# Attention values as 128 stationary columns (high beside low), with the two halves added in SBUF

## The chip, the cores and the metric

One core of a Trainium2 chip runs the whole program. The metric is the time of one execution on the device in microseconds (us): median 2431.57 us of 3 runs (2431.19 to 2432.11). TensorE is written PE (PEld is its weight load), VectorE DVE, ScalarE ACT, GpSimd POOL. Each engine takes its instructions from its own queue.

## The reference, cut to what matters

A two-layer decoder trunk on x (1, 256, 2048): retention, ConvFFN, sliding-window attention, ConvFFN, all in float32. The change is in the attention: 32 query heads of 64 columns share 4 key and value heads, two blocks of 128 tokens, window 128.

```
proj = h @ w_qkv + b_qkv; q, k, v = split(proj)
scores = q k^T * 64**-0.5 - slope * dist        (own block and the block before)
scores = where(valid, scores, -inf)
probs = softmax(concat(scores, sink))[..., :-1]
out = probs @ v;  return out @ w_out
```

## The kernel before, in words

Every wide product is made of three float32r products: an operand x is split in hi (x rounded to float32r) and lo = x - hi, and hi·hi, hi·lo and lo·hi are summed in PSUM. The weights come from HBM in units of 128 x 2048 (tile raw); ACT writes hi (L161), DVE writes lo (L162), 1024 columns at a time. PE runs the chunks of these units in one long stream: L267 and L269 for the projections that come out transposed, L256 to L258 for the others.

The rest is cut into generators ("tasks"). After each chunk `run_main` calls `split_ahead`, which may emit the next L161 and L162, and then `run_tasks`, which runs every task that is due, in order of due time. A task that yields n is due again n steps later (a step is one chunk of 512 columns, or two of 256). `tc.manual_schedule()` keeps the order of emission, so every engine's queue has the order in which this loop wrote it, and it does not depend on times.

Two query heads make a pair; 16 pairs, `att_pair`, come 4 steps apart: pairs 1 to 10 while the query columns 0 to 4 and the first output product run, pairs 11 to 16 while columns 5 to 7 and the second output product run. The stages of one pair, and the step in which they are emitted:

- step 0: scores on PE into two PSUM tiles (L679).
- step 1: DVE adds the ALiBi term and takes the maximum, with PSUM as input (L687), then L693 and L694.
- step 2: ACT takes the exponentials, four with their sums (L699), then L703.
- step 4: DVE adds the sink, inverts (L705, L706) and scales the probabilities (L710).
- step 6: PE transposes them, three per head into one PSUM tile each (L276); ACT and DVE split them into pT hi and lo (L400, L401).
- step 9: PE multiplies by the values into PSUM tile po (L393, inside `split_products`, called from `att_pair`), and ACT copies po to y (L731, L732).
- step 10: ACT and DVE split y into yT hi and lo (L400, L401).

Three pairs are under way at a time. In a stretch of 4 steps the queues hold, by the trace:

```
ACT: L731 L732 (pair n), L161, L400 yT (n), L400 pT x2 (n+1), L699 x4 and L703 (n+2), [L378], L161, [L638 x2]
DVE: L705 L706 L710 x4 (n+1), L687 x4 L693 L694 (n+2), L162, L401 yT (n), L401 pT x2 (n+1), [L379 L388], L162
```

In brackets: the eviction of a finished block of query columns (L378, L379, L388, L638), in every second stretch while query columns run. The PSUM tiles of this phase (`ms`, four slots) are taken in turn: two score tiles, po, two transpose tiles, and again.

`split_products` gives three matmuls, each with 64 stationary columns (one value head, hi or lo) and the probabilities as moving operand: for each head three of 256 moving columns (keys of block 0) and three of 128 (keys of block 1), 12 in all. `att_values` makes the values once, before the pairs.

Of the kernel before, what the change touches and what calls it, by code (L numbers as in the profile page):

```python
# [9 lines left out]
F32 = mybir.dt.float32  # L10
F32R = mybir.dt.float32r
AF = mybir.ActivationFunctionType
ALU = mybir.AluOpType
# [3 lines left out]
P = 128  # L17
D = 2048
S = 256
NT = S // P  # L20
# [3 lines left out]
KV = 4  # L24
GRP = 8
DH = 64
# [83 lines left out]
class Kernel:  # L110
# [533 lines left out]
    def att_values(self, at, g):  # L644
        v = self.ph.tile([P, NT, 256], F32, tag="qT", name="v", bufs=2)
        for t in range(NT):
            self.nc.vector.scalar_tensor_tensor(
                out=v[:, t], in0=g.ps[:, t, :256], scalar=self.r[:, t : t + 1], in1=self.bv,
                op0=ALU.mult, op1=ALU.add,
            )  # L650
        at["vs"] = x = self.ph.tile([P, 2, NT, 256], F32R, tag="vs", name="vs")
        self.nc.scalar.copy(out=x[:, 0], in_=v)
        self.nc.vector.tensor_tensor(
            out=x[:, 1], in0=v, in1=x[:, 0].bitcast(F32), op=ALU.subtract
        )

    def att_queries(self, at, b, g):
        qT = self.join(g, "qT", 2)
# [5 lines left out]
    def att_pair(self, at, qT, i, f):  # L664

        nc = self.nc
        kT, vs = at["kT"], at["vs"]
        jj = f // GRP
        al = self.ph.tile([P, 2, 384], F32, tag="al", name="al", bufs=2)
        nc.sync.dma_start(out=al, in_=self.a["alibi"][f])  # L670
        pr = self.ph.tile([P, 2, 384], F32, tag="pr", name="pr", bufs=3)
        soft = self.st.tile([P, 4, NT, 2], F32, tag="soft", name="soft")
        m, nm, es, den = (soft[:, x] for x in range(4))
        pss = [self.ms.tile([P, 512], F32, tag="ms", name="ms") for _ in range(2)]
        where = [slice(0, P), slice(P, P + S)]
        for t in range(NT):
            for s in range(2):
                rows = slice(s * DH, (s + 1) * DH)
                nc.tensor.matmul(  # L679
                    pss[s][:, where[t]], lhsT=qT[rows, i, t * P : (t + 1) * P],  # L680
                    rhs=kT[rows, jj, : (t + 1) * P], start=True, stop=True,
                )
        yield 1
        for s in range(2):
            sink = self.sinks[:, 2 * f + s : 2 * f + s + 1]
            for t in range(NT):
                nc.vector.tensor_tensor_reduce(  # L687
                    out=pr[:, s, where[t]], in0=pss[s][:, where[t]], in1=al[:, s, where[t]],
                    scale=DH**-0.5, scalar=sink, op0=ALU.add, op1=ALU.max,
                    accum_out=m[:, t, s : s + 1],  # L690
                )
        sk = self.sinks[:, 2 * f : 2 * f + 2].unsqueeze(1).broadcast_to([P, NT, 2])
        nc.vector.tensor_scalar_mul(nm, m, -1.0)  # L693
        nc.vector.tensor_tensor(out=es, in0=sk, in1=m, op=ALU.subtract)  # L694
        yield 1
        for s in range(2):
            for t in range(NT):
                x = pr[:, s, where[t]]
                nc.scalar.activation(  # L699
                    out=x, in_=x, func=AF.Exp, bias=nm[:, t, s : s + 1],  # L700
                    accum_out=den[:, t, s : s + 1],
                )
        nc.scalar.activation(out=es, in_=es, func=AF.Exp)  # L703
        yield 2
        nc.vector.tensor_tensor(out=den, in0=den, in1=es, op=ALU.add)  # L705
        nc.vector.reciprocal(den, den)  # L706
        for s in range(2):
            for t in range(NT):
                x = pr[:, s, where[t]]
                nc.vector.tensor_scalar_mul(x, x, den[:, t, s : s + 1])  # L710
        yield 2
        pTs = []
        for s in range(2):
            ps = self.ms.tile([P, 512], F32, tag="ms", name="ms")
            self.transposes(ps, [pr[:, s, n * P : (n + 1) * P] for n in range(3)])
            pT = self.ph.tile([P, 2, 384], F32R, tag="pT", name="pT", bufs=2)
            self.split_store(pT.unsqueeze(1), ps[:, :384].unsqueeze(1))
            pTs.append(pT)
        yield 3
        po = self.ms.tile([P, 2, S], F32, tag="ms", name="po")  # L720
        for s in range(2):
            vc = slice((2 * jj + s) * DH, (2 * jj + s + 1) * DH)
            pT = pTs[s]
            self.split_products(
                po[:DH, s], vs[:, :, 0, vc], pT[:, :, :S], start=True, stop=False
            )
            self.split_products(
                po[:DH, s, P:], vs[:, :, 1, vc], pT[:, :, S:], start=False, stop=True
            )
        y = self.ph.tile([P, S], F32, tag="y", name="y", bufs=2)  # L730
        nc.scalar.copy(out=y[:DH], in_=po[:DH, 0])  # L731
        nc.scalar.copy(out=y[DH:], in_=po[:DH, 1])  # L732
        yield 1
        self.attT[f] = x = self.ph.tile([P, 2, S], F32R, tag="yT", name="yT", bufs=12)
        self.split_store(x.unsqueeze(1), y.unsqueeze(1))

# [221 lines left out]
```

## Time and profile before

| | |
|---|---|
| profiled execution, its own time | 2431.45 us |
| its span, first to last instruction | 2429.3 us |
| PE busy, share of the span | 2413.0 us, 99% |
| DVE busy | 1554.9 us, 64% |
| ACT busy | 1224.6 us, 50% |
| POOL busy | 29.2 us, 1% |

The profile's chain of waits, followed back from the last instruction, has 97% of the span on PE. A busy PE is not PE at its peak, as matmuls are pipelined. Idle time of ACT or DVE costs nothing as long as PE is not waiting for them.

### The profile page before, as it was taken

The numbers are of one execution on the slowest core, as the hardware profiler recorded it, in microseconds if no ns is written. First come the engines' busy times: TensorE is split into PE (matmuls) and PEld (weight loads), VectorE is DVE, ScalarE is ACT, GpSimd is POOL, SyncE is SP. The second block draws the span as 40 slices with busy tenths as digits, with TensorE's granted clock in tenths as the row PEclk, the third lists the DMA queues.
The fourth block names the chain that finished last, engine by engine and source line by source line (L and its number), as shares of the span: only waits on it lengthen the run. The fifth ranks groups of instructions, "written<-read, shape, count | busy, mean of one in ns | idle before, by whom it ended". The sixth has DMA issues, their size and how long they took to land.

```text
span 2429.3 us, 31370 instructions
## 1 busy us (share of the span) xinstructions
PE 2413.0 (99%) x12676; PEld 2060.6 (85%) x12676; DVE 1554.9 (64%) x2104; ACT 1224.6 (50%) x1782; POOL 29.2 (1%) x37
## 2 busy tenths in 40 slices
PE   8999999999999999999999999999999999999998
PEld 7888888888888888888888888888888888888887
DVE  6555555554556775677577756876777477657774
ACT  6444344344445553555355545765555355535553
POOL 3000000000000000000000000000000000000000
PEclk9999999999999999999999999999999999999999
DMA  8655555555554555555555555445454555554553
GB/s 287 213 187 180 192 181 186 185 188 182 182 191 168 199 185 194 192 192 183 197 192 195 194 182 195 182 156 193 174 194 174 207 191 191 190 207 175 195 200 126
DMA packets 68977, 460.27 MB, mean 189 GB/s; under 512 B 8032, under 2 KB 9184, under 8 KB 16736
## 3 DMA queue, kind: packets, MB, share of 16 engines
q1 hardware_dynamic: 68544, 457.23, 52.7%
q8 instruction: 99, 1.62, 0.3%
q10 hardware_dynamic: 288, 1.05, 0.1%
q14 instruction: 46, 0.38, 0.0%
HBM read 456.15 MB, written 2.10 MB: 189 GB/s over the span
## 4 chain that ended last, share of the span: by engine, by line
PE 97%; DMA 1%; issue 1%; POOL 0%; DVE 0%; ACT 0%; SPq 0%; POOLq 0%; DVEq 0%; ACTq 0%
PE mm L267 33%; PE mm L269 17%; PE mm L256 13%; PE mm L258 12%; PE mm L257 12%; PE po L256 2%; PE po L258 2%; PE po L257 2%; PE po L393 1%; PE ms L276 1%; PE ms L679 1%; PE ms L503 0%; POOL acc L309 0%; DMA h<-in_xT 0%; DVE lo L162 0%
## 5 line engine op out<-in xcount | busy, mean ns | idle before, releaser
L162 DVE TENSOR_TENSOR lo<-raw,hi 128x1024 fp32r<-128x1024 f32 (+1 forms) x849 | 1018.4, 1219 | 612.3 <-ACT hi L161 611.9
L161 ACT CAST hi<-raw 128x1024 fp32r<-128x1024 f32 (+1 forms) x849 | 857.8, 1042 | 522.5 <-PE mm L258 332.3
L267 PE MATMUL mm<-xT,hi 128*128 128x512 f32 x3552 | 1107.9, 393 | 6.2 <-DVE xT L323 6.2
L269 PEld LDWEIGHTS mm<-xT,lo 128*128 128x128 f32 x3552 | 667.3, 188 | 150.3 <-DVE lo L162 3.1
L269 PE MATMUL mm<-xT,lo 128*128 128x256 f32 x3552 | 702.2, 279 | 1.1 <-DVE lo L162 1.0
L267 PEld LDWEIGHTS mm<-xT,hi 128*128 128x128 f32 x3552 | 540.5, 188 | 11.7 <-ACT hi L161 6.2
L256 PE MATMUL mm<-hi,zT 128*128 128x512 f32 x688 | 268.3, 390 | 0.0
L258 PE MATMUL mm<-hi,zT 128*128 128x512 f32 x688 | 267.7, 389 | 0.0
L257 PE MATMUL mm<-lo,zT 128*128 128x512 f32 x688 | 267.7, 389 | 0.0
L601 DVE SCALAR_TENSOR_TENSOR cv<-u,cw,cv 128x255 f32<-128x255 f32 x344 | 158.3, 481 | 6.1
L256 PE MATMUL mm<-hi,yT 128*128 128x512 f32 x384 | 153.3, 399 | 0.0
L258 PEld LDWEIGHTS mm<-hi,zT 128*128 128x128 f32 x688 | 129.1, 188 | 27.0
L257 PEld LDWEIGHTS mm<-lo,zT 128*128 128x128 f32 x688 | 129.2, 188 | 26.5
L256 PEld LDWEIGHTS mm<-hi,zT 128*128 128x128 f32 x688 | 129.1, 188 | 26.4
L258 PE MATMUL mm<-hi,yT 128*128 128x512 f32 x384 | 149.8, 390 | 0.0
L257 PE MATMUL mm<-lo,yT 128*128 128x512 f32 x384 | 149.7, 390 | 0.0
L378 ACT COPY u<-mm 128x512 f32<-128x512 f32 x86 | 50.4, 586 | 183.7 <-PE mm L269 183.7
L379 DVE TENSOR_TENSOR u<-mm,u 128x512 f32<-128x512 f32 x86 | 59.5, 692 | 93.2 <-ACT u L378 93.2
L594 ACT ACTIVATE cv<-u,cw 128x256 f32<-128x256 f32 x172 | 94.2, 595 | 48.7 <-DVE u L388 48.7
L611 ACT CAST zT<-cv 128x256 fp32r<-128x256 f32 x86 | 34.9, 406 | 156.2 <-DVE cv L609 156.2
L256 PE MATMUL mm<-hi,xT 128*128 128x512 f32 (+1 forms) x288 | 109.1, 379 | 0.0
L258 PE MATMUL mm<-hi,xT 128*128 128x512 f32 (+1 forms) x288 | 108.6, 377 | 0.0
(118 smaller groups left out, 1784.1 us busy)
## 6 DMA issues: line engine op xcount, KB each, us to landing
raw<-in_up SPq DMA_DIRECT2D x172, 1024.0 KB, 4.7
raw<-in_ret_in SPq DMA_DIRECT2D x94, 1024.0 KB, 4.8
raw<-in_dn SPq DMA_DIRECT2D x72, 1024.0 KB, 4.8
raw<-in_ret_out SPq DMA_DIRECT2D x32, 1024.0 KB, 4.7
raw<-in_qkv SPq DMA_DIRECT2D x20, 1024.0 KB, 4.7
raw<-in_att_out SPq DMA_DIRECT2D x14, 1024.0 KB, 4.7
raw<-in_dn SPq DMA_DIRECT2D x16, 512.0 KB, 3.2
raw<-in_dn SPq DMA_DIRECT2D x8, 768.0 KB, 4.3
```

The lines of the kernel that those rows point to most:

```text
L161: nc.scalar.copy(out=hi, in_=raw)
L162: nc.vector.tensor_tensor(out=lo, in0=raw, in1=hi.bitcast(F32), op=ALU.subtract)
L256: nc.tensor.matmul(out, lhsT=ah, rhs=hi, start=first, stop=False)
L257: nc.tensor.matmul(out, lhsT=ah, rhs=lo, start=False, stop=False)
L258: nc.tensor.matmul(out, lhsT=al, rhs=hi, start=False, stop=last)
L267: nc.tensor.matmul(out, lhsT=hi[:, sl], rhs=both, start=first, stop=False)
L269: nc.tensor.matmul(out[:, :S], lhsT=lo[:, sl], rhs=act[:, 0], start=False, stop=last)
L378: nc.scalar.copy(out=x, in_=g.ps[:, :, S:])
L379: nc.vector.tensor_tensor(out=x, in0=g.ps[:, :, :S], in1=x, op=ALU.add)
L594: nc.scalar.activation(out=c[:, half], in_=u[:, half], func=AF.Identity, scale=w[:, 2:3], bias=w[:, 3:4])
L601: nc.vector.scalar_tensor_tensor(out=c[:, half, d:], in0=u[:, half, : S - d], scalar=w[:, 2 - d : 3 - d], in1=c[:, half, d:], op0=ALU.mult ...
L611: nc.scalar.copy(out=z[:, 0], in_=s)
```

## The change

The values are laid out so that for each value head hi and lo stand side by side, 128 stationary columns: hi|lo for the first head of a pair, lo|hi for the second. One matmul with the hi of the probabilities and one with their lo replace three, so lo·lo is now summed as well. In po the hi part and the lo part of a head then stand in different halves of the partitions; ACT copies both (four copies of 64 x 256 where there were two) into the two halves of a y tile twice as wide, and DVE adds them in SBUF, in the task's next step, ahead of the split into yT. The values' own split is made in two pieces on each engine.

```diff
-        at["vs"] = x = self.ph.tile([P, 2, NT, 256], F32R, tag="vs", name="vs")
-        self.nc.scalar.copy(out=x[:, 0], in_=v)
-        self.nc.vector.tensor_tensor(
-            out=x[:, 1], in0=v, in1=x[:, 0].bitcast(F32), op=ALU.subtract
-        )
+        at["vs"] = x = self.ph.tile([P, NT, KV // 2, 4, DH], F32R, tag="vs", name="vs")
+        v = v.rearrange("p t (j s d) -> p t j s d", j=KV // 2, s=2)
+        for s in range(2):
+            self.nc.scalar.copy(out=x[:, :, :, 3 * s], in_=v[:, :, :, s])
+        for s in range(2):
+            self.nc.vector.tensor_tensor(
+                out=x[:, :, :, 1 + s], in0=v[:, :, :, s], in1=x[:, :, :, 3 * s].bitcast(F32),
+                op=ALU.subtract,
+            )
...
         for s in range(2):
-            vc = slice((2 * jj + s) * DH, (2 * jj + s + 1) * DH)
-            pT = pTs[s]
-            self.split_products(
-                po[:DH, s], vs[:, :, 0, vc], pT[:, :, :S], start=True, stop=False
-            )
-            self.split_products(
-                po[:DH, s, P:], vs[:, :, 1, vc], pT[:, :, S:], start=False, stop=True
-            )
-        y = self.ph.tile([P, S], F32, tag="y", name="y", bufs=2)
-        nc.scalar.copy(out=y[:DH], in_=po[:DH, 0])
-        nc.scalar.copy(out=y[DH:], in_=po[:DH, 1])
+            for m, (q, k) in enumerate(((slice(S), slice(S)), (slice(P, S), slice(S, S + P)))):
+                v = vs[:, m, jj, 2 * s : 2 * s + 2].rearrange("p x d -> p (x d)")
+                for x in range(2):
+                    nc.tensor.matmul(
+                        po[:, s, q], lhsT=v, rhs=pTs[s][:, x, k], start=m == 0 and x == 0,
+                        stop=m == 1 and x == 1,
+                    )
+        y = self.ph.tile([P, 2, S], F32, tag="y", name="y", bufs=2)
+        for s in range(2):
+            own, other = (slice(DH), slice(DH, P))[:: 1 - 2 * s]
+            nc.scalar.copy(out=y[own, 0], in_=po[own, s])
+            nc.scalar.copy(out=y[own, 1], in_=po[other, s])
         yield 1
+        nc.vector.tensor_tensor(out=y[:, 0], in0=y[:, 0], in1=y[:, 1], op=ALU.add)
+        y = y[:, 0]
         self.attT[f] = x = self.ph.tile([P, 2, S], F32R, tag="yT", name="yT", bufs=12)
         self.split_store(x.unsqueeze(1), y.unsqueeze(1))
```

## Rows read from the trace of the kernel before

**Rows 1.** The page's first part: busy time and share of each engine.
```profile
PE 2413.0 (99%) x12676; PEld 2060.6 (85%) x12676; DVE 1554.9 (64%) x2104; ACT 1224.6 (50%) x1782; POOL 29.2 (1%) x37
```

**Rows 2.** Busy time by window, over pairs 1 to 10; PEclk is the granted clock.
```profile
1520.00:1594.00 74.00, 74.00 (x483) 62.33 (x481) 65.35 (x189) 53.10 (x144) 0.00 (x0) 1.00 0.46 168
```

**Rows 3.** Timeline of ACT: start, us, line, operation, count, [idle before, releaser].
```profile
1521.10 0.37 ACT L731 COPY y<-po 64x256 f32<-64x256 f32 x1 [2.42 <-PE po L393]
...
1521.87 1.05 ACT L161 CAST hi<-raw 128x1024 fp32r<-128x1024 f32 x1
1522.82 0.40 ACT L400 CAST yT<-y 128x256 fp32r<-128x256 f32 x1
...
1523.87 0.41 ACT L699 ACTIVATE pr<-pr,soft 128x128 f32<-128x128 f32 x1
...
1525.73 0.57 ACT L378 COPY qT<-mm 128x512 f32<-128x512 f32 x1
...
1529.47 0.37 ACT L731 COPY y<-po 64x256 f32<-64x256 f32 x1 [0.78 <-PE po L393]
...
1537.85 0.37 ACT L731 COPY y<-po 64x256 f32<-64x256 f32 x1 [2.71 <-PE po L393]
...
1559.22 0.57 ACT L378 COPY qT<-mm 128x512 f32<-128x512 f32 x1
...
1631.43 0.57 ACT L378 COPY qT<-mm 128x512 f32<-128x512 f32 x1
...
1645.02 0.41 ACT L400 CAST yT<-y 128x256 fp32r<-128x256 f32 x1
```

**Rows 4.** The chain of waits in one pair: start us, us, engine, tile, line, count.
```profile
1520.02 1.05 PE po L393 x12
1521.06 0.52 PE mm L267 x2
1521.82 0.47 PE mm L267 x2
1522.29 0.24 PE mm L269 x2
1522.53 0.66 PE ms L276 x6
```

**Rows 5.** Timeline of DVE in the same stretch.
```profile
1522.95 1.22 DVE L162 TENSOR_TENSOR lo<-raw,hi 128x1024 fp32r<-128x1024 f32 x1
1524.09 0.42 DVE L401 TENSOR_TENSOR yT<-y,yT 128x256 fp32r<-128x256 f32 x1
...
1526.33 0.69 DVE L379 TENSOR_TENSOR qT<-mm,qT 128x512 f32<-128x512 f32 x1 [0.89 <-ACT qT L378]
...
1527.67 1.22 DVE L162 TENSOR_TENSOR lo<-raw,hi 128x1024 fp32r<-128x1024 f32 x1
...
1529.21 1.01 DVE L710 TENSOR_SCALAR pr<-pr,soft 128x128 f32<-128x128 f32 x4
1530.13 0.35 DVE L687 CUSTOM_DVE_ANT_0 pr<-ms,al,sinks 128x128 f32<-128x128 f32 x1
...
1530.81 0.35 DVE L687 CUSTOM_DVE_ANT_0 pr<-ms,al,sinks 128x128 f32<-128x128 f32 x1
...
1531.75 1.22 DVE L162 TENSOR_TENSOR lo<-raw,hi 128x1024 fp32r<-128x1024 f32 x1
```

**Rows 6.** Timeline of PE: value products and transposes at the ends of both runs.
```profile
1519.86 1.21 PE L393 MATMUL po<-pT,vs 128*64 128x256 f32 x12
...
1530.74 0.82 PE L276 MATMUL ms<-ident,pr 128*128 128x128 f32 x6
...
1588.83 0.82 PE L276 MATMUL ms<-ident,pr 128*128 128x128 f32 x6
...
1625.56 1.21 PE L393 MATMUL po<-pT,vs 128*64 128x256 f32 x12
...
1661.04 0.82 PE L276 MATMUL ms<-ident,pr 128*128 128x128 f32 x6
```

## The prediction

> **What bounds the kernel now.** I read the busy shares first, then the busy time by window over the attention, then the chain of waits, then the timelines of ACT, DVE and PE. PE is busy 99% of the span [rows 1], and in the attention pairs 74.00 of 74.00 us at a granted clock of 1.00, with DVE at 65 and ACT at 53 us [rows 2]. So what PE no longer does is won, and each us that PE has to wait is lost for good, since nothing behind it has slack to give back. The question is how near ACT and DVE are to being late. ACT's slack is written beside its copies of po: it stands idle for PE 0.78 us in a stretch that evicts query columns and 2.71 us in the next one, 3.49 us in two pairs [rows 3].
>
> **PE's part.** Now 12 matmuls of a pair take 1.05 us, that is 6 × (0.116 + 0.058) for 256 and 128 moving columns with 64 stationary ones; the wide matmuls behind them start with 0.52 in place of 0.47, their 128-column weights being late [rows 4]. After: 8 matmuls, four of 256 and four of 128 moving columns, all with 128 stationary columns. A 256-column one with such weights takes 0.24/2 = 0.12; a 128-column one is nearest to the transposes, 128 x 128, at 0.66/6 = 0.11 [rows 4], where the weight load sets the pace. Sum 4 × 0.12 + 4 × 0.11 = 0.92, last late load included, or 0.90 with 0.23 for two: against 1.10 a gain of 0.2 us a pair, 16 × 0.2 = 3.2 us. Ends: if the load cost nothing, the block would take 4 × 0.116 + 4 × 0.058 = 0.70, a gain of 0.35 us a pair and 5.6 in all; if all eight took 0.14, nothing. I take 3.2, as transposes have the shape of the new weights.
>
> The Trainium skill (TensorE: Matmul & The Clock Gate, Back-to-back issue gap) gives about 81 ns for a 128-column matmul in a stream with a load each. The transposes here took 110 ns. By the page the block would take 4 × 0.12 + 4 × 0.081 = 0.80 and the gain would be 4.8 us, the forecast 1.6 us lower.
>
> **ACT's and DVE's part.** Per pair: two more copies of 64 x 256, 0.77 us (1521.10 to 1521.87 for two [rows 3]); one addition of 128 x 256 on DVE, taken as 0.42 from the yT subtraction of that size [rows 5], between 0.35 (the smaller L687) and 0.69 (twice the columns, L379). The values' split in two pieces is made once and early: 0 to 0.5 us, estimated at a quarter more on each engine; its reader is the block at 1519.86 [rows 6]. No DMA is added. None of this would count by its busy time. What counts is a new wait: ACT's cast yT (L400) now waits for an addition on DVE, and that stands in DVE's queue where yT's subtraction stands now, behind a split L162 [rows 5], which itself waits for ACT's L161 just before the cast. Today the cast starts at 1522.82, as the L161 of 1521.87 ends [rows 3], and the L162 runs beside it.
>
> Queued behind the cast on ACT: two pT casts, the four exponentials, L703, in some stretches L378, and the next L161. For these wait DVE's next L162, and behind it L710 and L687, and for those PE's next transposes: L710 makes their input, and L687 has to finish reading the first score tile before the second transpose tile may take its PSUM slot. So the two engines, which ran beside each other, now run in turn. Followed by hand from pair 1, in us:
>
> - PE's block starts at 1519.86; the first copy follows 1.24 later now, 1.04 after: 1520.90.
> - Four copies 1.54, L161 1.05: 1523.48. L162 starts 0.02 later; the addition 1.14 after that (1522.95 to 1524.09 [rows 5]) and ends at 1525.07. Cast yT 1525.10, 2.3 later than now.
> - From cast to exponentials 1.05, from there to L378 1.86 [rows 3]: 1528.01. L379 0.60 later; L379 to L162 1.34: 1529.95; L162 to L687 2.46: 1532.41; the first head read 0.75 later (0.68 to the second head's start and its accumulator): pair 3's second transpose tile may start at 1533.2. PE is ready for it at 1530.74 + 0.33 - 0.4 = 1530.7 [rows 6]: PE's first stall, 2.5 us.
>
> From there DVE's queue has no gap for PE to catch up in, and a pair takes: L162 to the end of the addition 1.14 + 0.42; to the cast 0.03; to the exponentials 1.05; to the next L161 1.86; it and the handover 1.08; L162 to L687 2.46; L687 to the next L162 1.62 (1530.13 to 1531.75 [rows 5]). Sum 9.66 us, against 8.38 now (1529.47 to 1537.85 [rows 3]). With a query eviction, L378, L379 and L388 stand in place of the L161 on that path: 0.60 + 1.34 for 1.08, so 10.52. The copies are not in this sum: they fit beside DVE's work.
>
> Pairs 1 to 10: evictions lie ahead of pairs 3, 5 and 7 (first and third in rows 3, at 1525.73 and 1559.22). Pair 9's tile comes at 1533.2 + 4 × 9.66 + 2 × 10.52 = 1592.9; pair 10 has no scores behind it and waits for L710 alone (1.54 from L162, 1.01 long [rows 5]), 8.96 later: 1601.8. Now it starts at 1588.83 + 0.33 = 1589.2 [rows 6]: 12.7 late, in spite of nine gains of 0.2, so 14.5 us of stalls. Pairs 11 to 16: first copy at 1625.56 + 1.04 = 1626.6; with an eviction at 1631.43 pair 13 comes 12.3 later, at 1638.9; pair 14 9.66 later; from there no split lies ahead of yT (the cast at 1645.02 follows a copy [rows 3]), so 1.14 less: 8.52 and 7.82. Pair 16: 1664.9 against 1661.4 [rows 6], 3.5 late, so 4.5 us of stalls. After each run PE has no more of them. The last pair's yT comes up to 2.4 us later and is wanted soon by the output product; no row here prices that, so 0 to 2.4, taken as 0.
>
> Sum: 14.5 + 4.5 - 3.2 = +15.8. The profiled execution took 2431.45 us (span 2429.3), 0.12 below the median shown, which changes nothing: 2447.
>
> **The rivals.** (1) Only ACT's own time counts, and DVE is never the one that is late. ACT gets 0.77 of copies and about 1.7 of waiting a pair, 4.9 in two pairs, against a slack of 3.49 less 0.4 that PE runs ahead: 1.8 short in two pairs, 0.9 a pair, some 11 us over 12 pairs, less 3.2: 2439. For it: DVE's queue has gaps today. Against: each gap waits for ACT.
>
> (2) Not slower: the addition doesn't stand behind the split. It decides where the addition lies in DVE's queue. Ahead of that L162 it would cost ACT 0.4 in place of 1.6; with the copies 1.2 a pair, 2.4 in two, under the slack of 3.1. PE never waits and the gain stays: 2428, or 2426 with a weight load that costs nothing. For it: L687 frees DVE about when the copies end. Against: yT's own subtraction at 1524.09 follows the L162 of 1522.95 [rows 5], and the addition is emitted in the same task step.
>
> (3) Pauses of 1.5 to 2.5 us a pair make the granted clock fall; the rows show 1.00 in a stage without a pause. At the lower level PE's 8.2 us of work in a pair would take twice that; where it holds for 2 us of a pair, PE loses 1 us, which the next pause mostly takes up. I put it at up to 8 us: 2455.
>
> **How the numbers follow.** Forecast 2447, chance 0.68: its own range 2441 to 2453, from ±0.5 us a pair over 12 stalled ones, which covers an addition of 0.35 to 0.69. Rival 1: 0.15. Rival 2: 0.13. Rival 3: 0.04. The 8 in 10 range takes in rival 1 and part of the third: 2437 to 2454. Within 0.2% of 2431.6 means 2426.7 to 2436.4, about what a measurement of this kernel can tell from no change. Slower by more: forecast, rivals 1 and 3 less a part of rival 1 that lands low, 0.83. Within: 0.12. Faster: rival 2 with a cheap load, 0.05.
>
> **What would show it.** PE's eight matmuls at 0.9 us from first to next product; an addition on DVE that starts as an L162 ends; ACT idle some 1.6 us ahead of L400 yT, released by that addition; PE idle ahead of L276 of 1 to 2.5 us in pairs 3 to 10 and 13 to 16, released by DVE's L687 or L710; stretches of about 9.7 and 10.5 us. The forecast is wrong if PE stays without idle time between 1520 and 1594, or if the addition runs ahead of the split.

## The result, and the profile after

2449.71 us (median of 6 runs, 2448.51 to 2450.83) against 2431.48 before: a ratio of 1.0075, 95% interval 1.0062 to 1.0088. The change makes the kernel 18.2 us slower. The forecast was 2447.0, the 8 in 10 range 2437 to 2454. The profiled execution took 2448.51 us, its span is 2446.4. One of the 11 executions of a later version, the first that adds from PSUM, took 8636 us and is left out of that version's ratio.

The page's busy times and the head of its chain, as in [rows 1]:

```profile
PE 2416.9 (99%) x12612; PEld 2058.9 (84%) x12612; DVE 1561.5 (64%) x2121; ACT 1236.0 (51%) x1815; POOL 29.2 (1%) x37
...
PE 92%; DVE 3%; ACT 2%; issue 1%; DMA 1%; POOL 0%; SPq 0%; POOLq 0%; DVEq 0%; ACTq 0%
```

64 matmuls fewer, yet PE is "busy" 4 us longer and still at 99%: the first line hides the loss. In the second, PE's share of the chain has fallen from 97% to 92%, and DVE and ACT have taken the place. The same window as in [rows 2], and two shorter ones in it (columns: window, length, busy time and count of PE, PEld, DVE, ACT, POOL, granted clock, DMA share, GB/s):

```profile
1520.00:1594.00 74.00, 66.11 (x384) 53.09 (x383) 57.41 (x174) 51.21 (x140) 0.00 (x0) 0.98 0.38 138
1549.00:1551.00 2.00, 0.33 (x3) 0.12 (x1) 1.93 (x5) 1.55 (x5) 0.00 (x0) 1.00 0.17 66
1552.00:1555.00 3.00, 3.00 (x11) 2.61 (x11) 2.91 (x12) 0.81 (x1) 0.00 (x0) 0.50 0.00 0
```

PE is busy 66.11 of 74 us where it had no idle time before; 384 matmuls ran in it, 483 before; four a pair of the difference are the new form's. DVE and ACT are no busier than they were (57.41 and 51.21 against 65.35 and 53.10): nobody is overloaded, they wait for each other. The waits of the attention stage, 1480 to 1720 (total us, times, longest):

```profile
ACT yT L400 <- DVE y L742: 36.7, 16, 3.3
...
PE ms L276 <- DVE pr L715: 12.7, 10, 2.0
...
ACT y L739 <- PE po L730: 10.7, 6, 2.6
...
PE mm L256 <- ACT yT L400: 0.9, 1, 0.9
```

And the one that answers to the last but one, in the kernel before:

```profile
ACT y L731 <- PE po L393: 34.7, 16, 2.9
```

This pair of views is the case in short. Before, ACT waited for PE, 16 times in 16 pairs; that was its slack. Now it waits 16 times for the new addition, 36.7 us, and its wait for PE is left in only 6 pairs. The chain of waits through one pair (start, us, what):

```profile
1518.97 0.89 PE po L730 x8
1519.89 0.36 ACT y L739
1520.27 0.37 ACT y L740
1520.65 0.37 ACT y L739
1521.01 0.02 issue
1521.04 0.36 ACT y L740
1521.40 0.03 issue
1521.43 1.06 ACT hi L161
1522.51 1.23 DVE lo L162
1523.73 0.35 DVE y L742
1524.12 0.04 issue
1524.16 0.41 ACT yT L400
1524.56 0.76 ACT pT L400 x2
1525.32 1.75 ACT pr L704 x8
...
1529.01 1.22 DVE lo L162
```

Where [rows 4] had PE alone, the chain now goes from ACT's split to DVE's split, then to the addition behind it, then back to ACT. The cast that ACT started at 1522.82 before ([rows 3]; PE was then 1.04 us later than here) starts at 1524.16. The same on the two engines' timelines, with the idle time in brackets, ACT first:

```profile
1521.43 1.05 ACT L161 CAST hi<-raw 128x1024 fp32r<-128x1024 f32 x1
1524.16 0.41 ACT L400 CAST yT<-y 128x256 fp32r<-128x256 f32 x1 [1.68 <-DVE y L742]
...
1534.74 0.41 ACT L400 CAST yT<-y 128x256 fp32r<-128x256 f32 x1 [2.23 <-DVE y L742]
```

```profile
1522.51 1.23 DVE L162 TENSOR_TENSOR lo<-raw,hi 128x1024 fp32r<-128x1024 f32 x1 [0.67 <-ACT hi L161]
1523.65 0.42 DVE L742 TENSOR_TENSOR y<-y 128x256 f32<-128x256 f32 x1
1524.60 0.43 DVE L401 TENSOR_TENSOR yT<-y,yT 128x256 fp32r<-128x256 f32 x1 [0.53 <-ACT yT L400]
```

PE's value products and its stalls, as in [rows 6]; the transposes of pairs 3, 4, 5, 7 and 10:

```profile
1518.81 1.04 PE L730 MATMUL po<-pT,vs 128*128 128x256 f32 x8
...
1530.98 1.07 PE L276 MATMUL ms<-ident,pr 128*128 128x128 f32 x6 [1.46 <-DVE pr L715]
...
1540.70 1.07 PE L276 MATMUL ms<-ident,pr 128*128 128x128 f32 x6 [1.08 <-DVE pr L715]
...
1551.28 1.40 PE L276 MATMUL ms<-ident,pr 128*128 128x128 f32 x6 [1.96 <-DVE pr L715]
...
1571.57 1.07 PE L276 MATMUL ms<-ident,pr 128*128 128x128 f32 x6 [1.15 <-DVE pr L715]
...
1600.64 1.16 PE L276 MATMUL ms<-ident,pr 128*128 128x128 f32 x6 [1.97 <-DVE pr L715]
```

L715 is L710 of the kernel before, L692 is L687, L704 is L699: the new lines moved them down by five. From pair 3 on PE waits for the scaling of the probabilities (of pairs 3 to 10 only pair 6 does not, for a reason told in the last section), and the distance of these starts (9.72 us from pair 3 to 4, 10.58 to pair 5) is set by ACT and DVE.

**How the loss is added up.** I take the start of the same PE work in both traces. Profiles differ by up to 3 us in the first 92 us of the kernel, and from there to the attention two traces keep the same distance (here PE is 1.04 us earlier than before, at 91 as at 1477), so each figure is the shift less the shift at 1477. Value product of pair 1: 0, so the values' split in two pieces costs PE nothing. Of pair 10: +13.2 us. Of pair 16: 3.5 more. Behind the last yT: 1.4 more. Sum 18.1 at the end of the stage, and it stays at that to the last matmul: nothing was given back.

### The profile page after: what moved, and what is told of

Same layout as the page of the kernel before. It is cut to its first block, busy times and chain, and to the rows that moved or that the text cites. A ratio compares the mean times of both kernels' runs of the same rounds, so it can differ in the third digit from the quotient of the medians.

```text
span 2446.4 us, 31283 instructions
## 1 busy us (share of the span) xinstructions
PE 2416.9 (99%) x12612; PEld 2058.9 (84%) x12612; DVE 1561.5 (64%) x2121; ACT 1236.0 (51%) x1815; POOL 29.2 (1%) x37
## 3 DMA queue, kind: packets, MB, share of 16 engines
q10 hardware_dynamic: 288, 1.05, 0.1%
## 4 chain that ended last, share of the span: by engine, by line
PE 92%; DVE 3%; ACT 2%; issue 1%; DMA 1%; POOL 0%; SPq 0%; POOLq 0%; DVEq 0%; ACTq 0%
PE mm L267 32%; PE mm L269 16%; PE mm L256 12%; PE mm L258 12%; PE mm L257 12%; PE po L258 2%; PE po L256 2%; PE po L257 2%; DVE lo L162 1%; PE ms L276 1%; ACT pr L704 1%; PE po L393 1%; ACT hi L161 1%; DVE pr L692 1%; PE ms L503 0%
## 5 line engine op out<-in xcount | busy, mean ns | idle before, releaser
L162 DVE TENSOR_TENSOR lo<-raw,hi 128x1024 fp32r<-128x1024 f32 (+1 forms) x849 | 1018.2, 1218 | 615.4 <-ACT hi L161 614.9
L161 ACT CAST hi<-raw 128x1024 fp32r<-128x1024 f32 (+1 forms) x849 | 857.8, 1042 | 519.7 <-PE mm L258 330.4
```

What stands on the lines that cost most here:

```text
L161: nc.scalar.copy(out=hi, in_=raw)
L162: nc.vector.tensor_tensor(out=lo, in0=raw, in1=hi.bitcast(F32), op=ALU.subtract)
```

## The experiments

Each was timed beside the kernel before on the same chip, in three groups, and the ratios are to its time there: 2431.2 us for the versions without the addition, with the wait alone, on POOL and with a step between; 2430.92 for the addition 8 columns wide and the second version that adds from PSUM; 2431.08 for the other four. Theory: the cast of yT waits on ACT for an addition that stands behind a 1.2 us split on DVE, and this one wait turns two engines side by side into two in turn. Rival A: ACT has too much work with two more copies. Rival B: the loss lies in DVE's additional work, or in the new form of the product. Rival C: any wait of ACT for another engine's addition costs the same, whatever stands ahead of it. Rival D: the clock.

**Without the addition.** y's hi half goes straight to the split.

```diff
         yield 1
-        nc.vector.tensor_tensor(out=y[:, 0], in0=y[:, 0], in1=y[:, 1], op=ALU.add)
         y = y[:, 0]
```

> The changed kernel without the addition (it leaves out one half of each value product): eight matmuls and four copies stay. Theory (the cast of yT waits for an addition that stands behind a split on DVE): the wait goes, and with it all stalls of PE ahead of L276; what stays is 16 gains of 0.16 us on PE: 2429 us, within 1. Rival A (the two further copies make ACT late): still 4 us or more above before, over 2435. Rival B (128 stationary columns cost PE the time): still about 2449.

Measured 2431.15 us, ratio 0.9999 (0.999 to 1.0008). The 18 us are gone with the addition, with all four copies and the eight matmuls in place. But I had expected PE's gain to show, 2 us more. The trace says where it went (pair 3, PE and DVE):

```profile
1531.46 0.09 DVE L692 DVE_READ_ACCUMULATOR2_ANT soft<- 128x1 f32 x1
...
1531.60 0.55 PE L276 MATMUL ms<-ident,pr 128*128 128x128 f32 x3 [0.66 <-DVE soft L692]
```

The second transpose tile starts 1.15 us behind the first, where 0.33 is usual, as it waits for the score tile that DVE's L692 still reads. This costs 0.8 us each in pairs 3 and 5, and small delays in later pairs bring it to the whole gain of 2.6 us. That the copies are what makes L692 late is tried below.

**Without the addition and without the two copies.** The halves that only the addition needs are not copied.

```diff
-            nc.scalar.copy(out=y[own, 1], in_=po[other, s])
         yield 1
-        nc.vector.tensor_tensor(out=y[:, 0], in0=y[:, 0], in1=y[:, 1], op=ALU.add)
```

> The changed kernel without the addition and without the two copies that it needs (it leaves out one half of each value product); eight matmuls. The run without the addition alone took 2431.15 us, not 2429. Theory: the two further copies put ACT 0.77 us later in the stretches with a query eviction and took back PE's gain there; without them PE's 16 x 0.16 us show: 2428.5 to 2429 us. Rival: the gain is lost elsewhere (128 stationary columns, the value split): 2431.

Measured 2429.1 us, 0.9991 (0.9983 to 1.0). PE over the whole stage:

```profile
1480.00:1720.00 240.00, 239.98 (x1386) 201.77 (x1385) 177.70 (x423) 156.20 (x357) 0.69 (x1) 1.00 0.50 180
```

No idle time, and PE's lead grows by 0.16 us with nearly each value product, to 2.1 us at the end. So the eight matmuls are worth something, and in the kernel without the addition the two copies of 0.37 us took it back by pushing ACT, and behind it L692, over the edge in the stretches with a query eviction.

**The wait alone, in the old kernel.** The kernel before, with one DVE operation of y with itself that changes no value, in the place of the addition: twelve matmuls, two copies.

```diff
         yield 1
+        nc.vector.tensor_tensor(out=y, in0=y, in1=y, op=ALU.max)
```

> The kernel before, with one DVE instruction more in each pair: y becomes max(y, y), in the place where the change adds. 64 stationary columns, two copies. Theory: this alone brings the whole loss, since DVE and ACT set the pace and not PE or the copies: 2448 to 2451 us, with stretches of 9.7 and 10.5 us. Rival A (the copies carry a good part): 2440 or less. Rival B (the weights): 2432.

Measured 2447.85 us, 1.0065 (1.0053 to 1.0078): one operation of 0.42 us per pair, 6.7 us in all, costs 16.7. Its rows for ACT's wait and PE's stalls (pairs 5, 6 and 7):

```profile
ACT yT L400 <- DVE y L734: 45.9, 16, 4.1
```

```profile
1552.06 1.07 PE L276 MATMUL ms<-ident,pr 128*128 128x128 f32 x6 [1.79 <-DVE pr L710]
1561.79 1.07 PE L276 MATMUL ms<-ident,pr 128*128 128x128 f32 x6 [0.94 <-DVE pr L710]
1572.37 1.06 PE L276 MATMUL ms<-ident,pr 128*128 128x128 f32 x6 [1.10 <-DVE pr L710]
```

They come 9.73 and 10.58 us apart, the pace of the changed kernel. Neither the product's form nor the copies are needed for the loss. Nor is the clock (rival D): it is granted at 1.00 over the whole stage here.

**The two extra copies taken out, the addition kept.** The hi half is added to itself.

```diff
-            nc.scalar.copy(out=y[own, 1], in_=po[other, s])
...
-        nc.vector.tensor_tensor(out=y[:, 0], in0=y[:, 0], in1=y[:, 1], op=ALU.add)
+        nc.vector.tensor_tensor(out=y[:, 0], in0=y[:, 0], in1=y[:, 0], op=ALU.add)
```

> The changed kernel with the addition (of the hi half to itself: it leaves out the other half) but without the two further copies. Theory: DVE and ACT in turn set the pace, and the copies lie beside DVE's work, so only the first pair of each run and the last pair's end become 0.77 us earlier: 2446.5 to 2448.5 us, some 2 us under the change. Rival A (the copies carry a good part of the loss): 2440 or less.

Measured 2449.68 us, 1.0076 (1.0063 to 1.009), the time of the changed kernel. I had expected some 2 us less; 12.3 us of copies are gone from ACT and next to nothing is won, because ACT spends the time waiting for the addition instead (45.8 us in this trace, 36.7 in the changed kernel). The first stall is shorter, as expected (0.83 us against 1.46), but a stretch takes 9.84 us in this trace against 9.72: the first cast of pT follows the cast of yT by 0.43 us here and by 0.31 in the changed kernel. At the end of the stage 1.1 us are left of the copies in the two traces, which the medians do not show. Rival A is dead.

**The addition on POOL.** An engine with an empty queue.

```diff
-        nc.vector.tensor_tensor(out=y[:, 0], in0=y[:, 0], in1=y[:, 1], op=ALU.add)
+        nc.gpsimd.tensor_tensor(out=y[:, 0], in0=y[:, 0], in1=y[:, 1], op=ALU.add)
```

> The changed kernel with the addition on POOL, which is idle there. Theory: POOL's addition of 128 x 256 (0.75 us or more, by L309's rows at the start of the kernel) runs beside ACT's L161 of 1.05 us, behind no split, so the cast of yT waits for at most 0.5 us: no stalls of PE or few: 2429 to 2431 us. Rival C (any wait of ACT for another engine's addition costs the same, whatever stands ahead of it): 2445 or more. Rival A: over 2435.

Measured 2430.4 us, 0.9998 (0.9989 to 1.0007). All engines around one addition:

```profile
1520.38 0.36 ACT L740 COPY y<-po 64x256 f32<-64x256 f32 x1
...
1520.77 1.05 ACT L161 CAST hi<-raw 128x1024 fp32r<-128x1024 f32 x1
...
1520.82 0.74 POOL L742 TENSOR_TENSOR y<-y 128x256 f32<-128x256 f32 x1 [47.98 <-ACT y L740]
...
1521.72 0.40 ACT L400 CAST yT<-y 128x256 fp32r<-128x256 f32 x1
```

It takes 0.74 us in place of 0.42, but starts as the fourth copy ends and lies wholly beside ACT's L161, so the cast is not late. A slower engine, and the kernel is 19 us faster than the changed one. Rival C is dead as well: the cast waits for another engine's addition here too, and it costs nothing.

**The addition earlier on DVE.** In the step of the copies, so that it stands between L715 and L692 and not behind the split.

```diff
-        yield 1
         nc.vector.tensor_tensor(out=y[:, 0], in0=y[:, 0], in1=y[:, 1], op=ALU.add)
+        yield 1
```

> The changed kernel with the addition emitted straight after the copies, in the same step. On DVE it then stands ahead of the split L162, but also ahead of L692, the scores' first DVE work (L687 before). Theory, followed by hand: the cast of yT no longer waits, but DVE now waits for PE's value product and four copies before it can read the scores: from the product's start 1.04 + 1.53 + 0.4 to L692 and 0.8 to the freed PSUM tile make 3.8 us, where PE wants the tile after 2.6: a stall of about 1.1 us in 12 pairs, 13 us less 2.6: 2441 to 2444 us, PE's idle time inside L276 (before its second tile). Rival, the prediction's second one (ahead of the split the addition costs nothing): 2428 to 2431 us.

Measured 2430.17 us, 0.9996 (0.9987 to 1.0004). My expectation was wrong by nearly 11 us at its near end; the prediction's second rival had it right. The rows, pair 3, ACT, PE and DVE:

```profile
1528.76 0.37 ACT L740 COPY y<-po 64x256 f32<-64x256 f32 x1
...
1528.87 0.87 PE L276 MATMUL ms<-ident,pr 128*128 128x128 f32 x6
...
1529.16 0.42 DVE L741 TENSOR_TENSOR y<-y 128x256 f32<-128x256 f32 x1
...
1529.50 0.34 DVE L692 CUSTOM_DVE_ANT_0 pr<-ms,al,sinks 128x128 f32<-128x128 f32 x1
...
1529.77 0.48 DVE L692 CUSTOM_DVE_ANT_0 pr<-ms,al,sinks 128x256 f32<-128x256 f32 x1
```

I had reasoned that L692, made late by the addition, would hold the score tile that the second transpose tile needs. Here all six transposes are done by 1529.74, while L692 reads its first score tile until 1530.25: that tile is not what PE waits for. In this build the second transpose tile carries a wait for ACT instead, and starts 0.08 us after the fourth copy of po ends: it takes po's place in PSUM, not the score tile's.

**A step between the addition and the split.** The addition stays where the change put it, the cast of yT comes one step later.

```diff
         nc.vector.tensor_tensor(out=y[:, 0], in0=y[:, 0], in1=y[:, 1], op=ALU.add)
+        yield 1
```

> The changed kernel with one more step between the addition and the split into yT, so that ACT comes to the cast after the exponentials. Theory: the addition still stands behind L162 on DVE, but is long done when ACT gets to the cast; no stalls ahead of L276, 2429 to 2431 us; the last pair's yT is later and PE may wait up to 3 us for it once, 2432 to 2434 then. Rival C: 2445 or more. Rival A: over 2435.

Measured 2432.72 us, 1.0005 (0.9996 to 1.0014): the wait is harmless once ACT has something else to do first. What remains is the stall of pairs 3 and 5 (0.66 us each in this trace, as without the addition) and the last pair's yT, for which PE waits 0.6 us in one piece and loses 1.4 in all.

**An addition 8 columns wide.** In its place, but with most of its work left out.

```diff
-        nc.vector.tensor_tensor(out=y[:, 0], in0=y[:, 0], in1=y[:, 1], op=ALU.add)
+        nc.vector.tensor_tensor(out=y[:, 0, :8], in0=y[:, 0, :8], in1=y[:, 1, :8], op=ALU.add)
```

> The addition stays where the change put it, but is 8 columns wide in place of 256, so most of it is left out. Theory (place: ACT's cast waits for whatever stands behind the split on DVE): the addition falls from 0.42 to between 0.10 and 0.15 us, and a stalled pair's stretch of 9.72 us gets shorter by that alone: 0.27 to 0.32 x 13 stalled pairs = 3.5 to 4.2 us of 18: 2445.5 to 2446.5, at most 2447.5. Rival (length: DVE is late because it has more work): with the work gone the time comes back, 2431 to 2435.

Measured 2446.85 us, 1.0067 (1.0054 to 1.0079). Its group in the list of lines, 1519 to 1594 (busy us, mean ns | idle before):

```profile
L742 DVE TENSOR_TENSOR y<-y 128x8 f32<-128x8 f32 x8 | 1.3, 158 | 0.0
```

A thirty-second of the columns takes 158 ns in place of 420 and keeps 16 of the 18 us, a little above the 2445.5 to 2446.5 of the theory and below its limit. Rival B is dead: it is not the work on DVE, it is the place in its queue.

**Two versions that add from PSUM.** ACT copies only the two hi halves; DVE adds the lo halves from po. In the first, the additions come in the step behind the copies and the split one more step later (the last pair without a step between); in the second, in the step of the copies, but for two pairs. The lines that these replace are left out here.

```diff
+        y = self.ph.tile([P, S], F32, tag="y", name="y", bufs=2)
+        halves = [(slice(DH), slice(DH, P)), (slice(DH, P), slice(DH))]
+        for s, (own, other) in enumerate(halves):
+            nc.scalar.copy(out=y[own], in_=po[own, s])
+        if f < 15:                # second version: if f in (8, 14):
+            yield 1
+        for s, (own, other) in enumerate(halves):
+            nc.vector.tensor_tensor(out=y[own], in0=po[other, s], in1=y[own], op=ALU.add)
         yield 1
```

> Same result as the change with ACT's work as it was before: ACT copies only the two hi halves, DVE adds the lo halves from PSUM in two operations of 64 x 256, and the split into yT comes one step later (for the last pair the additions come straight after the copies instead). Theory: no wait of ACT for a split, no further copies, so no stalls and PE's gain stays: 2428.5 to 2429.5 us, a little under the kernel before. Rival (more DVE work in a stretch with a query eviction makes L162 and L715 late): 2431 or more.

> ACT copies only the two hi halves, and DVE adds the two lo halves straight from PSUM, in the step of the copies and so ahead of the split that it stands behind in the changed kernel; for two pairs, the 8th and the 14th by number f, one step later. Theory (place): DVE's two additions (0.86 us each for 64 x 256 with PSUM as input, in psum_add) fit ahead of the split, ACT has the old number of copies, and PE keeps the 2.6 us of its shorter products: 2428.5 to 2429.5. Rival (the additions make DVE late for the scores, as in psum_add, or hold po too long): 2430.5 or more, with idle time of PE ahead of transposes.

Measured 2430.47 us, 0.9995 (0.9986 to 1.0004), and 2433.38 us, 1.0009 (1.0 to 1.0019). Both missed: I hoped to keep PE's gain, and neither keeps the whole of it. (The 0.86 us that the second expectation gives to each addition is the time of the two together, so DVE has less to do than it says; that makes the miss worse.) In the second, pair 3:

```profile
1530.63 0.86 DVE L743 TENSOR_TENSOR y<-po,y 64x256 f32<-64x256 f32 x2
...
1531.64 0.52 PE L276 MATMUL ms<-ident,pr 128*128 128x128 f32 x3 [0.50 <-DVE y L743]
```

Now the additions are po's last reader, and the second transpose tile waits for them by name: this shows directly that in this build it takes po's place. PE loses 0.50, 0.50, 0.27 and 0.28 us in pairs 3, 5, 8 and 9. An addition that holds a PSUM slot is no better than a copy that holds it. What takes the gain back in the first version was not tried.

None of the versions beats the kernel before by more than 0.2%. The fastest that computes the whole is level with it (2430.17 against 2431.08); the ceiling is the version without addition and copies, 2 us below. Differences of this size are near the noise of the medians, but the traces resolve them. At the end of the stage, less the shift at 1477, the versions stand against the kernel before as follows (us):

| version | shift |
|---|---|
| no addition, no extra copies | -2.1 |
| addition earlier; from PSUM, first version | -0.8 |
| no addition; addition on POOL | 0.0; 0.1 |
| a step between | +1.4 |
| from PSUM, second version | +2.1 |
| the wait alone, in the old kernel | +16.2 |
| addition 8 columns wide | +16.3 |
| extra copies out, addition kept | +17.1 |
| the change | +18.1 |

## Why the prediction was right

**PE's part: 3.2 us forecast, 2.6 measured, and in the changed kernel worth little.** From the first matmul of a value product to the next product's first it is 1.05 us before and 0.88 after; with the late load behind it, which is in both traces, 0.17 a pair against the 0.2 forecast, 2.6 in 16 pairs where PE is not held up (2.1 were left in the run without addition and copies). By single starts the four 256-column matmuls take 0.53 us and the four 128-column ones 0.35. I had 0.48 and 0.44: the sum was good by luck, as the two errors go opposite ways. One gap behind a 256-column matmul is 0.17 where the others are 0.12, and those behind the 128-column ones are 0.06 and 0.11 in turn. The four take 88 ns each on average, where I had 110 from the transposes. The Trainium skill (TensorE: Matmul & The Clock Gate, Back-to-back issue gap) gives about 81 ns for this width in a stream with a load each. That is nearer than my 110, but by the page the block would have taken 0.80 us, and it took 0.88; the one long gap of 0.17 makes 0.05 of the difference. That late weights make the 0.17 was not tried. In the changed kernel the gain counts only in the pairs in which PE is not paced by the others; elsewhere PE reaches its next stall sooner and waits longer.

**The new wait: right in place and size.** The addition starts as the split L162 ends and takes 0.42; ACT stands idle for it 1.68, 2.23 and 3.27 us in the first three stalled stretches. The single-cause runs bear it out from both sides: the wait alone brings 16.7 of 18.2 us, and the addition taken out, put on POOL, put ahead of the split, or followed by a step takes the loss away. By the traces 1.9 us lie between the wait alone and the change; 1.1 of them are gone in the run without the extra copies, and the rest was not tried apart.

**The loop: 9.66 and 10.52 us forecast, 9.72 and 10.58 measured.** From transposes to transposes, pairs 3 to 10: 9.72, 10.58, 10.06, 10.23, 9.72, 9.72, 9.63, together 69.7 against 68.6 forecast. The third and fourth have a fall of the clock in them (below) and make up for each other.

**The step that failed: "L687 has to finish reading the first score tile before the second transpose tile may take its PSUM slot".** In the changed kernel PE waits for the scaling L715 with its first transpose tile, in every stalled pair, and in pairs 3 to 9 the second tile carries a wait for ACT's copies of po; it starts at 1531.49, 0.06 us after the fourth copy ends and 0.7 before L692 is done with the first score tile (1532.2). Pair 3, the fourth copy, the first two of the second tile's three matmuls, and L692's second half of the first score tile:

```profile
1531.07 0.36 ACT L740 COPY y<-po 64x256 f32<-64x256 f32 x1
...
1531.49 0.45 PE L276 MATMUL ms<-ident,pr 128*128 128x128 f32 x2
...
1531.74 0.48 DVE L692 CUSTOM_DVE_ANT_0 pr<-ms,al,sinks 128x256 f32<-128x256 f32 x1
```

I took the turn of the four slots from the kernel before and held it for fixed. It differs from build to build: the second transpose tile waits for the score tile before, without the addition, with it on POOL and with a step between, and for po's readers in the changed kernel and where the addition stands early. It can differ within one build too: in the old kernel with the wait it carries the wait for ACT in pairs 3 to 9, and in pair 15 it waits 0.69 us for L687. The pace came out right all the same, because DVE runs L692 ahead of its next split whoever waits for it. What the wrong step did to the sum: the first stall is 0.7 us earlier than forecast (second tile at 1531.49 + 1.04 = 1532.5 on the old clock, forecast 1533.2), and the last stretch is 0.67 longer, since I took its 0.70 off for a change of releaser that isn't there. That these two cancel is luck: pair 10 is 13.2 late, forecast 12.7. In the experiment with the early addition nothing cancelled, and the same step made me miss by 11 us.

**The second run of pairs: 3.5 forecast, 3.7 measured** (3.5 above is less pair 10's own gain of 0.17). Behind it, the last pair's yT, the term that was mis-sized: bounded by 0 and 2.4 and taken as 0. PE waits 0.90 us for it in one piece by the row above, and with smaller delays 1.6 are lost, 1.4 less pair 16's own gain. So 0.5 in the first run, 0.2 in the second and 1.6 behind it make 2.3 of the 2.7 by which the forecast was low; the rest is rounding and the distance of profiled runs from medians.

**The rivals.** Only ACT's time (2439): refuted by the run without the extra copies, which is as slow. The addition ahead of the split (2428): refuted for the change by the order of the rows, and confirmed as a mechanism, at 2430, where the addition was really put there; the prediction had all of PE's gain kept there, and its trace keeps 0.8 us: 0.7 are lost at pair 10, where PE waits for L715, and the rest mostly in small delays of the second transpose tile behind the copies. The clock (2455): it does fall once in the attention, and costs nothing, as shown below.

## What to carry to other kernels

An operation of 0.4 us, made 16 times on an engine that is busy two thirds of the time, cost 18 us, because another engine's queue waits for it and it stands behind a long operation which itself waits for that other engine: price a new cross-engine step by what stands ahead of it in its queue and what stands behind its reader, not by its length or by the engine's busy share. What took the loss away here: an engine with an empty queue (even a slower one), a place ahead of the long operation, or a step between producer and reader. And before a step of an argument rests on which PSUM slot a tile takes, look for that wait in the trace of the build at hand: a build with one operation moved may take another.

## What the runs showed of the hardware

- The granted clock of TensorE falls to 0.50, its level of 1.2 GHz, for 3.41 us in the changed kernel, as PE takes up work again after its pause of 1.96 us ahead of pair 5 (windows above: PE busy 0.33 of 2 us at 1.00, then 0.50). Pauses of 1.97 us in the same trace, ahead of pair 10, and of 1.79 and 1.86 in the old kernel with the wait, brought no fall, while 1.69 and 1.86 in the kernel with the narrow addition each did; so the length of the pause alone does not decide, and what does was not tried.
- The fall cost nothing. From pair 5's transposes to pair 7's it is 20.29 us with it (1551.28 to 1571.57) and 20.31 in the old kernel with the wait, where the clock stayed at 1.00 (1552.06 to 1572.37). The scores came later by the fall, and the next pause, 0.94 us there, was gone here: this stage, paced by ACT and DVE, took up the slower PE.
- The addition of 128 x 256 in SBUF takes 0.74 us on POOL and 0.42 on DVE, 8 columns of it 0.16 on DVE.
